# Row maxima of dense attention: two heads' products of 64 rows beside each other in the array, one reduction over two banks

## The chip, the cores and the metric

The kernel runs on one core of a Trainium2 chip. The metric is the device time of one execution in microseconds. A core has five engines that run side by side and wait for each other by semaphores: TensorE (PE in the profile; its weight loads are listed apart as PEld), VectorE (DVE), ScalarE (ACT), GpSimd (POOL) and SyncE (SP). Each takes its instructions in the order in which the program lists them. DMA transfers are issued by SP or by POOL, and then run by themselves.

## The reference, cut to what matters

One layer of an encoder over 1024 positions: a projection, two kinds of attention side by side, an output projection and a gated feed-forward part. The change lies in the dense attention (8 query heads in two groups of 4; each group shares one key head of 64 elements):

```
def block(qb):
    sc = jnp.einsum('bqkgd,bskd->bkgqs', qb, k, preferred_element_type=jnp.float32) * scale
    p = jax.nn.softmax(sc, axis=-1)
    return jnp.einsum('bkgqs,bskd->bqkgd', p.astype(v.dtype), v)
o = lax.map(block, qg)
```

A softmax gives the same result whatever is taken off all scores of a row. The kernel takes off an approximate maximum of the row, so that the exponentials stay in range; the maximum itself is not part of the output.

## The kernel before, in words

The work runs in stages: the input projection in four chunks of columns, the dense attention, the windowed attention, the output projection, and the feed-forward part. Operands of TensorE are in a 4-byte format that keeps fewer digits than float32; so a number is split into a high part and a low part, and a product is made of up to three products of parts.

Dense attention is worked in 16 groups: 8 blocks of 128 queries by 2 key heads (`a_main`, from line 594 on). A group has 4 query heads, and goes over the 1024 keys in 8 key tiles of 128. For each key tile there are two 512-column products for the scores (L609 with the keys, high parts over low parts in the 128 rows, against the queries; L610 with the high parts of the keys and rows of -1 against the low parts of the queries and the row maxima, which subtracts them), an exponential on ACT (L612), and four products in float32 with the values (L604, each of which shows as two records in the trace), two key tiles later.

The row maxima of a group have to be there before its scores, so they are made one group ahead, by the steps of `a_prep` (from line 567 on), of which `a_main` takes one behind most key tiles (`plan`, line 1006). The first step transposes the queries of the group into `q2`: their high parts stand in rows 0 to 63 and again in rows 64 to 127. Then come four steps `mx(i)`, one for each head, and `last`, which joins the maxima of the two halves of the keys and transposes them into the operand of L610. In `R_K2A` the rows 0 to 63 hold the high parts of the keys and the rows 64 to 127 their low parts. So the product of L582 is the high part of the queries times the whole of the keys, 128 rows deep, with 512 keys in one bank of the accumulator memory. Each bank is reduced to a maximum for each row by one DVE instruction (L583). The first group uses four banks in turn; the others, which share the memory with the scores, use banks 0 and 1.

The operands of the keys are made in `k_ready` (lines 315 to 327) during the last chunk of the projection: `kv_fetch` loads the keys, ACT and DVE split them (L319, L320), TensorE transposes them (L176), and ACT copies them to `R_K2A` (L326) and their high parts alone to rows 0 to 63 of `R_KHA` (L327). The rows 64 to 127 of `R_KHA` hold -1. In the loop over the 28 products of the projection (L393 to L395 are its three products of parts), `k_ready` of the last keys is called behind the product that is called 6, and the four `mx` of the first group behind the product that is called 3. A scheduler then sets the order of each engine's instructions by the dependencies and by its own notion of how long things take. So the `mx` of the first group end up between the projection's products, and those of the other groups between the products of scores and values. POOL works in the same stretch on additions of the projection's outputs (L405), rotary steps (L284), and the loads of two tables (L648).

## Time and profile before

| what | us |
|---|---|
| median of 3 runs (1378.29 to 1380.36) | 1379.73 |
| the profiled execution | 1379.28 |
| its span from first to last instruction | 1377.5 |
| PE busy in the span | 1319.2 |
| the products of the maxima (L582) start from, to | 228.6, 434.1 |
| the reductions (L583) start from, to | 230.0, 434.6 |

The dense stage is some 205 of the span's 1377.5 us. A row of a group gives the line, the engine, the operation, output and input with their shapes, the count, the busy time, the mean length in ns of one, and then the idle time of the engine ahead of these instructions with what ended it. A row in order of time gives the start, the length, the engine, the line and the count; the lengths of products are modelled and overlap, so what a product takes is read from the distance of the starts.

### The profile page before, as it was taken

The numbers are of one execution on the slowest core, as the hardware profiler recorded it, in microseconds if no ns is written. First come the engines' busy times: TensorE is split into PE (matmuls) and PEld (weight loads), VectorE is DVE, ScalarE is ACT, GpSimd is POOL, SyncE is SP. The second block draws the span as 40 slices with busy tenths as digits, with TensorE's granted clock in tenths as the row PEclk, the third lists the DMA queues.
The fourth block names the chain that finished last, engine by engine and source line by source line (L and its number), as shares of the span: only waits on it lengthen the run. The fifth ranks groups of instructions, "written<-read, shape, count | busy, mean of one in ns | idle before, by whom it ended". The sixth has DMA issues, their size and how long they took to land.

```text
span 1377.5 us, 20282 instructions
## 1 busy us (share of the span) xinstructions
PE 1319.2 (96%) x7559; PEld 1141.6 (83%) x7559; DVE 988.2 (72%) x1634; ACT 671.5 (49%) x1066; POOL 515.3 (37%) x388
## 2 busy tenths in 40 slices
PE   7898989999999999999998999999999999999998
PEld 6798989989999887887886788888888888888887
DVE  5986586774445677688558888778777888586664
ACT  7744634554445656666344444444444445244331
POOL 2754354130001566651036455665565552200000
PEclk9999999999999999989999999999999999999999
DMA  7035303100000223234322222333223225797973
GB/s 245 16 116 138 78 9 87 30 9 1 1 1 9 83 71 102 82 109 137 107 70 84 91 94 92 102 112 112 103 100 115 85 100 176 280 293 239 295 232 112
DMA packets 117956, 148.61 MB, mean 108 GB/s; under 512 B 48809, under 2 KB 74849, under 8 KB 117857
## 3 DMA queue, kind: packets, MB, share of 16 engines
q1 hardware_dynamic: 116705, 144.17, 32.2%
q0 software_dynamic: 1152, 3.15, 0.9%
q8 instruction: 59, 0.97, 0.3%
q14 instruction: 40, 0.33, 0.1%
HBM read 113.47 MB, written 33.82 MB: 107 GB/s over the span
## 4 chain that ended last, share of the span: by engine, by line
PE 75%; DVE 12%; issue 3%; ACT 2%; POOL 1%; DMA 1%; DVEq 0%; ACTq 0%; SPq 0%; POOLq 0%
PE ps L1123 10%; PE ps L1124 9%; PE ps L1125 9%; PE ps L604 7%; PE ps L1239 5%; PE ps L1237 5%; PE ps L1238 5%; PE ps L609 2%; PE ps L582 2%; PE ps L847 2%; DVE bigf L707 2%; PE ps L610 2%; PE ps L849 2%; PE ps L848 2%; PE ps L393 2%
## 5 line engine op out<-in xcount | busy, mean ns | idle before, releaser
L1123 PE MATMUL ps<-bigr 128*128 128x512 f32 x616 | 241.7, 392 | 6.1 <-DVE bigf L1127 5.8
L1125 PE MATMUL ps<-bigr 128*128 128x512 f32 x616 | 240.5, 390 | 0.0
L1124 PE MATMUL ps<-bigr 128*128 128x512 f32 x616 | 240.2, 390 | 0.0
L1106 ACT ACTIVATE bigr<-bigf 128x512 fp32r<-128x512 f32 x154 | 93.0, 625 | 157.3 <-POOL bigf L1098 97.5
L1155 DVE SCALAR_TENSOR_TENSOR bigf<-bigf 128x768 f32<-128x768 f32 (+1 forms) x176 | 145.5, 885 | 27.0 <-ACT bigf L1153 27.0
L604 PEld LDWEIGHTS ps<-bigf 128*128 128x128 f32 x1024 | 138.7, 191 | 10.1
L1123 PEld LDWEIGHTS ps<-bigr 128*128 128x128 f32 x616 | 115.9, 188 | 34.5 <-DVE bigf L1127 10.0
L1217 ACT ACTIVATE bigr<-bigf 128x1024 fp32r<-128x1024 f32 x77 | 80.7, 1060 | 119.4 <-PE ps L1239 65.6
L393 PE MATMUL ps<-bigr 128*128 128x256 f32 x448 | 128.9, 288 | 7.8 <-ACT bigf L408 5.2
L1125 PEld LDWEIGHTS ps<-bigr 128*128 128x128 f32 x616 | 116.1, 188 | 24.3
L1107 DVE TENSOR_TENSOR bigr<-bigf,bigr 128x512 fp32r<-128x512 f32 x110 | 113.1, 1043 | 31.3 <-ACT bigr L1106 31.2
L1124 PEld LDWEIGHTS ps<-bigr 128*128 128x128 f32 x616 | 116.0, 188 | 23.5
L604 PE MATMUL ps<-bigf 128*128 128x65 f32 x1024 | 135.3, 267 | 0.0
L583 DVE TENSOR_REDUCE bigf<-ps 128x1 f32<-128x512 f32 x128 | 85.8, 689 | 64.7 <-PE ps L582 63.1
L394 PE MATMUL ps<-bigr 128*128 128x256 f32 x448 | 128.3, 287 | 0.0
L395 PE MATMUL ps<-bigr 128*128 128x256 f32 x448 | 128.1, 286 | 0.0
L612 ACT ACTIVATE bigf<-ps 128x512 f32<-128x512 f32 x128 | 76.0, 597 | 101.3 <-PE ps L610 99.7
L1238 PE MATMUL ps<-bigr 128*128 128x512 f32 x308 | 119.9, 389 | 0.0
L1237 PE MATMUL ps<-bigr 128*128 128x512 f32 x308 | 119.8, 389 | 0.0
L1239 PE MATMUL ps<-bigr 128*128 128x512 f32 x308 | 119.8, 389 | 0.0
L1218 DVE TENSOR_TENSOR bigr<-bigf,bigr 128x1024 fp32r<-128x1024 f32 x77 | 93.0, 1221 | 26.9 <-ACT bigr L1217 24.8
L1169 POOL TENSOR_TENSOR bigf<-bigf 128x512 f32<-128x512 f32 x44 | 69.1, 1591 | 90.3 <-DVE bigf L1160 66.0
(209 smaller groups left out, 3048.4 us busy)
## 6 DMA issues: line engine op xcount, KB each, us to landing
bigf<-w_down SPq DMA_DIRECT2D x99, 256.0 KB, 4.1
bigf<-w_up SPq DMA_DIRECT2D x44, 512.0 KB, 3.6
bigf<-gscr SPq DMA_DIRECT2D x77, 256.0 KB, 4.3
gscr<-bigf SPq DMA_DIRECT2D x33, 512.0 KB, 2.6
bigf<-w_in SPq DMA_DIRECT2D x8, 1024.0 KB, 6.7
bigf<-x SPq DMA_DIRECT2D x15, 512.0 KB, 8.0
bigf<-tmx SPq DMA_DIRECT2D x8, 672.0 KB, 5.0
bigf<-w_out SPq DMA_DIRECT2D x8, 512.0 KB, 3.6
```

The costliest lines, as they stand in the source:

```text
L393: mm(o, ah, wh, start=(k == 0 and t % 2 == 0 and n != 2), stop=False, skip_group_check=True)
L394: mm(o, ah, wl, start=False, stop=False, skip_group_check=True)
L395: mm(o, al, wh, start=False, stop=(k == 3), skip_group_check=True)
L604: mm(bank(ob, 65, 66 * i), f(slots[kt] + 128 * i, 128), f(F_VA + 132 * kt + 66 * kv, 65), start=(kt == 0 and i == 0), stop=(kt == 7), skip ...
L1107: (gp if n in (2, 4) else vec).tensor_tensor(rp(o + 512, [128, 4], [1, 128]), src, rfp(o, [128, 4], [1, 128]), op=OP.subtract)
L1123: mm(bank(b), wh, th, start=(k == 0 and n in (1, 5, 6, 7)), stop=False, skip_group_check=True)
L1124: mm(bank(b), wh, tl, start=False, stop=False, skip_group_check=True)
L1125: mm(bank(b), wl, th, start=False, stop=(k == 3), skip_group_check=True)
L1155: vec.scalar_tensor_tensor(f(a + o, n), f(i + d, n), w_, f(a + o, n), op0=OP.mult, op1=OP.add)
L1237: mm(o, ah, r(d, 512), start=(q == 0 and n in (1, 5, 2)), stop=False, skip_group_check=True)
L1238: mm(o, ah, r(d + 1024, 512), start=False, stop=False, skip_group_check=True)
L1239: mm(o, al, r(d, 512), start=False, stop=(q == NQ - 1), skip_group_check=True)
```

## The change

The step `mx(i)` is made anew. It now takes a pair of heads and one half of the keys. It issues two products of 64 rows: one with rows 0 to 63 of `q2` for the first head of the pair and rows 0 to 63 of `R_K2A`, the other with rows 64 to 127 of `q2` for the second head (where the same high parts stand again) and rows 64 to 127 of a new operand `R_KK`. Both use the high parts of the keys alone. They write two neighbouring banks, and one reduction over both gives two maxima for each row. The count of products stays 128, that of the reductions goes from 128 to 64. `R_KK` is filled by a copy of 512 KB, from rows 0 to 63 of `R_KHA` to rows 64 to 127, on POOL's queue, behind the last `k_ready`.

```
+R_KK = R_KHA + 2048
...
         def mx(i):
-            for hf in range(2):
-                b = 2 * (i % 2) * (g == 0) + hf
-                mm(bank(b), r(q2 + 128 * i, 128), r(R_K2A + 1024 * kv + 512 * hf, 512), start=True, stop=True)
-                vec.tensor_reduce(f(SM_MC + 8 * hf + i, 1), bank(b), axis=AX.X, op=OP.max)
+
+            pair, hf = divmod(i, 2)
+            b = 2 * (i % 2) * (g == 0)
+            for u, k in ((0, R_K2A), (1, R_KK)):
+                rows = slice(64 * u, 64 * u + 64)
+                mm(bank(b + u), r(q2 + 128 * (2 * pair + u), 128)[rows], r(k + 1024 * kv + 512 * hf, 512)[rows],
+                   start=True, stop=True)
+            vec.tensor_reduce(f(SM_MC + 8 * hf + 2 * pair, 2), heads(PS[:, 512 * b:512 * b + 1024], 2), axis=AX.X,
+                              op=OP.max)
...
             for u in range(2, 4):
                 k_ready(u)
                 v_ready(u)
+            gp.dma_start(r(R_KK, 2048)[64:128], r(R_KHA, 2048)[0:64])
```

The order of instructions changes at three places. Lines of the changed kernel lie 1 higher than those of before up to the dense stage's `a_prep` and 6 higher behind it (7 behind the copy): L394 to L396 are the projection's products (L393 to L395 before), L586 is the product of a maximum (L582), L615 and L616 are the scores (L609 and L610), L610 the product with the values (L604), L406 and L285 are L405 and L284.

The first place is PE near the end of the projection, where the first group's maxima stand. Before, around the second and third step of the maxima:

```order
L394 MATMUL ps<-bigr 128x256
L582 MATMUL ps<-bigr 128x512 [waits DVE_49]
L582 MATMUL ps<-bigr 128x512
L395 MATMUL ps<-bigr 128x256
L393 MATMUL ps<-bigr 128x256
L582 MATMUL ps<-bigr 128x512 [waits DVE_49]
```

In the changed kernel, around the second product of the first pair; the semaphore named DMASW0 is that of POOL's DMA queue:

```order
L394 MATMUL ps<-bigr 128x256
L586 MATMUL ps<-bigr 128x512 [waits DMASW0_49]
L586 MATMUL ps<-bigr 128x512 [waits DVE_49,Activation_49]
L586 MATMUL ps<-bigr 128x512
L395 MATMUL ps<-bigr 128x256
L396 MATMUL ps<-bigr 128x256
```

The first product of the first pair stands ten projection products ahead of these rows, at the place where the first two L582 stood before; the second product has moved behind those ten, and now waits for the copy, and the rest of the projection's products stand behind it.

The second place is POOL at the same time. Before, behind the two additions of the projection's outputs:

```order
L477 TENSOR_TENSOR bigf<-bigf 128x512 [waits DVE_49,Pool_49]
L405 TENSOR_TENSOR bigf<-bigf 128x4x256 [waits DVE_49]
L405 TENSOR_TENSOR bigf<-bigf 128x4x256 [waits Activation_49]
L284 TENSOR_TENSOR bigf<-bigf 128x8x16 [waits DVE_49,Pool_49]
L284 TENSOR_TENSOR bigf<-bigf 128x8x16
```

In the changed kernel:

```order
L478 TENSOR_TENSOR bigf<-bigf 128x512 [waits DVE_49,Pool_49]
L406 TENSOR_TENSOR bigf<-bigf 128x4x256 [waits DVE_49]
L406 TENSOR_TENSOR bigf<-bigf 128x4x256 [waits Activation_49]
L996 DMA bigr<-bigr 64x2048 [waits PE_49,Activation_49]
L285 TENSOR_TENSOR bigf<-bigf 128x8x16 [waits DVE_49,Pool_49]
```

The copy (L996) stands behind both additions, and ahead of the rotary steps; nothing else on POOL has moved here.

The third place is PE in a later group of the dense stage. Before, from one step of the maxima on:

```order
L582 MATMUL ps<-bigr 128x512
L604 MATMUL ps<-bigf 128x65 x2
L582 MATMUL ps<-bigr 128x512
L604 MATMUL ps<-bigf 128x65 x2
L609 MATMUL ps<-bigr 128x512
L610 MATMUL ps<-bigr 128x512
L582 MATMUL ps<-bigr 128x512
L604 MATMUL ps<-bigf 128x65 x2
```

In the changed kernel, from one pair to the next:

```order
L586 MATMUL ps<-bigr 128x512 x2
L615 MATMUL ps<-bigr 128x512
L616 MATMUL ps<-bigr 128x512
L610 MATMUL ps<-bigf 128x65 x4
L615 MATMUL ps<-bigr 128x512
L616 MATMUL ps<-bigr 128x512
L610 MATMUL ps<-bigf 128x65
L586 MATMUL ps<-bigr 128x512 x2
```

Before, the two products of a step mostly stood apart, with products of the values between them; now the two of a pair stand together, with two score products twice and five products of the values (ten records) up to the next pair.

## The prediction

> **What bounds the kernel now.** I read the page first, then the busy time by stretches of the span, then the instructions in order of time in the dense stage, and last the groups and waits of the lines that the change touches. The page gives the engines for the whole span; the stretches (columns: from:to, length, then busy time and count of PE, PEld, DVE, ACT and POOL, granted clock, DMA share, GB/s) tell the stages apart.

> ```profile
> PE 1319.2 (96%) x7559; PEld 1141.6 (83%) x7559; DVE 988.2 (72%) x1634; ACT 671.5 (49%) x1066; POOL 515.3 (37%) x388
> 260.00:300.00 40.00, 39.50 (x281) 35.91 (x281) 31.80 (x54) 23.58 (x38) 8.93 (x3) 1.00 0.01 2
> 300.00:340.00 40.00, 40.00 (x289) 36.67 (x288) 21.36 (x38) 18.83 (x33) 2.38 (x2) 1.00 0.03 8
> 340.00:380.00 40.00, 40.00 (x288) 36.63 (x288) 19.02 (x37) 18.82 (x33) 0.00 (x0) 1.00 0.01 1
> ```

> The dense stage is bound by TensorE alone: PE is busy for all of 300 to 380 at full clock, while DVE works half of it. Here the weight loads (PEld) are close behind, at 92%. So a saving on DVE is worth nothing here, and one on PE is worth its whole size. One stretch of PE in order of time shows what a maximum costs (start, length, engine, line):

> ```profile
> 300.89 0.48 PE L609 MATMUL ps<-bigr 128*128 128x512 f32 x1
> 301.21 0.40 PE L582 MATMUL ps<-bigr 128*128 128x512 f32 x1
> 301.44 0.39 PE L610 MATMUL ps<-bigr 128*128 128x512 f32 x1
> 301.67 1.00 PE L604 MATMUL ps<-bigf 128*128 128x65 f32 x8
> 302.48 0.48 PE L609 MATMUL ps<-bigr 128*128 128x512 f32 x1
> 302.80 0.39 PE L610 MATMUL ps<-bigr 128*128 128x512 f32 x1
> 303.03 1.00 PE L604 MATMUL ps<-bigf 128*128 128x65 f32 x8
> 303.83 0.48 PE L609 MATMUL ps<-bigr 128*128 128x512 f32 x1
> ```

> Start to start is what a product takes from PE; the lengths overlap. The key tile from 300.89 to 302.48 holds one maximum product (L582) and takes 1.59 us; the next, from 302.48 to 303.83, has none and takes 1.35. So one product costs 0.24 us, though its modelled length is 0.39, and two cost 0.48. A record of L604 takes 0.10 (eight in 0.81). The first 512-column product behind them takes 0.32 instead of 0.23, about 0.1 more: its own weight load was not hidden.

> **The change part by part.**

> *The reductions.* 128 of one bank become 64 of two:

> ```profile
> L583 DVE TENSOR_REDUCE bigf<-ps 128x1 f32<-128x512 f32 x128 | 85.8, 689 | 64.7 <-PE ps L582 63.1
> L464 DVE TENSOR_REDUCE bigf<-bigf 128x16 f32<-128x1024 f32 x4 | 4.8, 1212 | 0.0
> 301.64 0.69 DVE L583 TENSOR_REDUCE bigf<-ps 128x1 f32<-128x512 f32 x1 [0.66 <-PE ps L582]
>   DVE bigf L583: 2.7, 6
> ```

> The last row is of the products' own line: PE sat idle ahead of L582 for 2.7 us, 6 times, until a reduction had ended. A reduction over 1024 elements takes 1.21 us on another line, so 64 of them take 77.6 us against 88.2 (128 x 0.689): 10.6 us less on an engine that waited 63.1 us for these very products. Worth nothing on the path. On the other side, both banks now come free together, at 0.43 (product's start to reduction, 301.21 to 301.64) + 0.1 + 1.21 = 1.75 us behind a pair's start. In the new order two pairs have some 2.1 us of other PE work between them (two L609, two L610 and ten L604 by the lines of before), so no wait follows. Where DVE is fuller, at 260 to 300, PE may wait longer than the 2.7 us that it lost to reductions before; I take 0, and keep 2.7 more as the bound.

> *The products.* Their number stays 128, but each uses 64 of the array's rows, in two halves. If the halves stream together, a pair takes 0.24 instead of 0.48, and 64 pairs save 64 x 0.24 = 15.4 us. What stands against it is that every neighbour of a pair uses all 128 rows, so the array changes its division into a pair and out of it again: about 128 times. The trace of before has one such change, at its start, where a transposition of 8 rows (L512) follows those of 128 rows:

> ```profile
> 6.04 0.42 PE L179 MATMUL ps<-bigf 128*128 128x128 f32 x1
> 6.39 0.18 PEld L512 LDWEIGHTS ps<-bigf 8*128 8x128 f32 x1 [0.33 <-issue]
> 6.39 0.27 PE L512 MATMUL ps<-bigf 8*128 8x8 f32 x1
> 5.83 0.23 PEld L179 LDWEIGHTS ps<-bigf 128*128 128x128 f32 x1
> 5.83 0.63 PE L179 MATMUL ps<-bigf 128*128 128x128 f32 x2
> 16.58 1.04 PE L179 MATMUL ps<-bigf 128*128 128x128 f32 x8
> ```

> The weights of the product at 6.04 had been loaded from 5.83 on, ahead of it. Those of L512 were not loaded ahead: they began at 6.39, 0.35 us behind the start of the product before and 0.07 before its modelled end at 6.46, and the profile names nothing else that L512 waited for. It is a single event, at a place where the kernel has just begun, but the nearest row there is. Carried over to a 512-column product with a length of 0.39: the next weights start at 0.32, a load takes about 0.1, and the next product streams at 0.42 or 0.43 instead of 0.23 or 0.24. That is a hold of 0.19 at each change. A pair then costs 0.24 for the stream, 0 to 0.10 for the second half's weights, and 2 x 0.19: 0.62 to 0.72 against 0.48, so 0.14 to 0.24 more. Times 64: 9 to 15 us; I take 12. The change pays only if a hold is under about 0.1 us.

> [...]

> *The copy of the keys.* It is issued on POOL behind two additions, and PE's order has the second product of the first pair wait for it, with all of PE's later work behind.

> ```profile
> 223.12 5.81 POOL L405 TENSOR_TENSOR bigf<-bigf 128x1024 f32<-128x1024 f32 x2 [5.65 <-DVE bigf L405]
> DMA to landing us min/median/max: 3.7/4.1/4.4
> bigf<-w_up SPq DMA_DIRECT2D x44, 512.0 KB, 3.6
> bigf<-x SPq DMA_DIRECT2D x15, 512.0 KB, 8.0
> 228.61 0.63 PE L582 MATMUL ps<-bigr 128*128 128x512 f32 x2
> 229.08 0.28 PE L393 MATMUL ps<-bigr 128*128 128x256 f32 x1
> 229.19 0.27 PE L394 MATMUL ps<-bigr 128*128 128x256 f32 x1
> ```

> The two additions end at 223.12 + 5.81 = 228.93, so the copy can't be issued earlier, though the keys themselves are ready before. The only loads on POOL's queue, L648 with 384 KB, land in 3.7 to 4.4 us (second row); loads of 512 KB on the other queue take 3.6 (w_up) to 8.0 (x, in a crowd at the start). No copy from on-chip memory to on-chip memory is in the trace. With 4.1 it lands at 233.0. PE is at the first pair at 228.61; one product (0.24) and ten projection products at 0.12 later, at about 230.05, it stands at the product that waits. It is idle until 233.0: 3.0 us, from 2.5 to 6.8 by the other rows. What was late before is no cover, since PE ran without a gap through this place. The reductions of this group follow as they did, and end (four of 1.21) before PE needs their result behind some 40 more projection products. Behind the copy on POOL stand the rotary steps L284 and the table loads; half a microsecond of issue there delays nothing that PE waits for.

> A pause on PE can also cost clock:

> ```profile
> 203.42 0.54 PE L176 MATMUL ps<-bigr 128*128 128x128 f32 x4 [1.71 <-DVE bigr L320]
> 207.55 0.72 PE L176 MATMUL ps<-bigr 128*128 128x128 f32 x4 [3.60 <-DVE bigf L191]
> 208.41 0.41 PE L394 MATMUL ps<-bigr 128*128 128x256 f32 x1
> 208.63 0.41 PE L395 MATMUL ps<-bigr 128*128 128x256 f32 x1
> 208.00:212.00 4.00, 4.00 (x21) 4.00 (x20) 3.35 (x6) 2.45 (x5) 0.44 (x1) 0.50 0.25 66
> ```

> After gaps of 1.71 and 3.60 us the granted clock was 0.50, and some 20 products came 0.21 apart (208.41 to 208.63) instead of 0.12: about 2 us. One gap of 3.0 is shorter than that, so I take 0 and keep 2 as a bound.

> *Sum.* The profiled execution took 1379.28 us with a span of 1377.5; the median of the runs is 1379.73, 0.45 above it. 1379.28 + 12 for the changes of division + 3.0 for the copy = 1394 us. The case's own range: 1379.3 + 9 + 2.5 = 1391 at its low end, and 1379.3 + 15 + 6.8 + 2 + 2.7 = 1406 with every bound at once.

> **The rivals.**

> *The halves stream together and a change of division costs nothing.* Faster. For it: the weights of a half could load while the other half streams, and the product before a pair is a 512-column one in about half of the places, long enough for both loads. Price: -15.4 + 3.0 = 1367 us; with 0.10 per pair for the second half's weights, -9.0 + 3.0 = 1373. Take 1370. Against it: the row of L512. It decides from a hold under 0.1 us per change, and at 0.07 the gain just pays for the copy: 64 x (0.24 - 0.05 - 0.14) = 3.

> *The halves do not overlap.* Then the change doesn't do what it says: each 64-row product takes 0.24 as before, without a hold, and only the copy is left: 1382 us, 0.2% slower. For it: nothing in this trace shows two products at once. Against it: nothing either.

> *The hold is that of L512 in full,* 0.35 at each change on top of the stream and the loads (0.10 each): 0.24 + 0.10 + 2 x 0.35 = 1.04 per pair, 0.56 more, 64 x 0.56 + 3 = 39 us: 1418. Against it: the transpositions there started 0.21 apart (5.83 and 6.04), while later eight of them take 1.04 in all, 0.1 apart, so that stretch ran slow.

> **How the numbers follow.** Forecast (holds of about 0.19 and the copy): 0.53, around 1394. Free changes of division: 0.29, around 1370. No overlap and no hold: 0.08, around 1382. Full hold: 0.06, around 1418. Holds of 0.07 or so, which about cancel: 0.04, around 1380. The range from 1367 to 1406 takes in the first, the second and those between, and leaves out the full hold and the crossing of several bounds. About 0.2% is what a measurement of this kernel can tell from no change, 2.8 us. Faster by more: 0.29. Within it: the cancelling case and part of the no-overlap case, 0.07. Slower: 0.64.

> **What would show it right or wrong.** In the profile after: the weight loads of each pair, and those of the product behind it, start only near the modelled end of the product before, 0.3 us and more behind its start; key tiles with a pair take 0.6 to 0.7 us more than those without, not 0.24; a gap of about 3 us in PE near 230, ended by the copy; DVE's reductions at about 1.2 us and DVE no busier. The prediction is wrong if the second product of a pair starts within hundredths of the first and the next full product 0.24 later (first rival), if the products of a pair are 0.24 apart with no hold (second), or if the copy has landed before PE asks for it.

## The result, and the profile after

| | before | changed |
|---|---|---|
| median, us | 1380.05 | 1457.72 |
| lowest of the runs, us | 1378.29 | 1457.24 |
| profiled execution, us | 1379.28 | 1457.24 |
| its span, us | 1377.5 | 1455.5 |
| mean granted clock of TensorE | 0.988 | 0.942 |

The changed kernel is slower: ratio 1.0562, interval 1.0547 to 1.0578, which is 77.7 us. The forecast was 1394, with a range up to 1406: the sign is right, the size is not. (One of the four executions of the changed kernel took 1569.5 us at a mean clock of 0.866 and is left out of the ratio.)

The page of the changed kernel, engines and granted clock in 40 slices:

```profile
PE 1390.2 (96%) x7559; PEld 1181.9 (81%) x7559; DVE 981.4 (67%) x1570; ACT 674.1 (46%) x1066; POOL 514.7 (35%) x389
PEclk9999997555799999999999999999999999999999
```

PE's share of the span is 96% as before, with the same 7559 instructions. By the busy share alone nothing has happened. The second row tells what has: from the seventh slice on, five slices of 36 us each with a lower clock, three of them at half clock throughout. Before, no slice is under 8. The stretches of the dense stage of the changed kernel, cut where the granted clock changes and at two round places (the clock is the third number from the right):

```profile
205.20:212.00 6.80, 5.03 (x25) 5.06 (x26) 5.41 (x13) 5.08 (x10) 1.03 (x1) 0.50 0.12 39
232.50:242.70 10.20, 9.98 (x39) 8.01 (x40) 4.97 (x5) 0.00 (x0) 1.15 (x2) 0.50 0.24 61
249.60:382.70 133.10, 132.47 (x490) 108.49 (x491) 48.84 (x65) 39.00 (x63) 15.93 (x15) 0.50 0.04 10
340.00:380.00 40.00, 40.00 (x152) 33.15 (x152) 9.17 (x13) 10.06 (x18) 0.00 (x0) 0.50 0.00 1
382.70:460.00 77.30, 77.30 (x534) 64.67 (x532) 33.07 (x44) 35.40 (x60) 0.00 (x0) 1.00 0.00 1
420.00:460.00 40.00, 40.00 (x279) 33.71 (x277) 18.01 (x24) 17.47 (x30) 0.00 (x0) 1.00 0.00 1
```

The stretch at 205.2 is there before as well (6.8 us from 205.7). The other two are new: 10.2 us from 232.5, and 133.1 us from 249.6. In 40 us at half clock PE issues 152 products, at full clock 279 (before: 288). PE is "busy" for all of both.

Where the 77.7 us lie in the kernel is told by the exponentials, which run through the whole dense stage (lengths, then the first and the last start). Before, and then in the changed kernel:

```profile
L612 ACT ACTIVATE bigf<-ps x128: 582/597/602, 239.4 to 453.1; 128x512 f32<-128x512 f32 x128
```

```profile
L618 ACT ACTIVATE bigf<-ps x128: 589/597/602, 246.6 to 529.8; 128x512 f32<-128x512 f32 x128
```

Up to the first exponential 7.2 us are lost, from the first to the last 283.2 - 213.7 = 69.5, and behind the last 1455.5 - 529.8 - (1377.5 - 453.1) = 1.3. That is the whole difference of the spans, 78.0. The loss is in the stage that the change is in, and in what leads up to it.

Next, the price of the change at full clock. DVE joins the maxima once in each group; the distance of two joins is the time of a group. Before, and then in the changed kernel behind 382.7:

```profile
327.88 0.17 DVE L586 TENSOR_TENSOR bigr<-bigf 128x4 fp32r<-128x4 f32 x1
341.33 0.17 DVE L586 TENSOR_TENSOR bigr<-bigf 128x4 fp32r<-128x4 f32 x1
```

```profile
429.69 0.17 DVE L592 TENSOR_TENSOR bigr<-bigf 128x4 fp32r<-128x4 f32 x1
443.71 0.17 DVE L592 TENSOR_TENSOR bigr<-bigf 128x4 fp32r<-128x4 f32 x1
```

13.45 against 14.02 (13.43 over several groups of before): 0.59 more in a group, 0.147 for each of its four pairs, 9.4 us in 16 groups. (The line numbers differ between the kernels: the join is L586 before and L592 in the changed kernel, where L586 is the product of a pair.) PE in order of time shows both halves of it in the changed kernel:

```profile
427.48 0.48 PE L615 MATMUL ps<-bigr 128*128 128x512 f32 x1
427.88 0.51 PE L586 MATMUL ps<-bigr 64*128 64x512 f32 x2
428.32 0.50 PE L616 MATMUL ps<-bigr 128*128 128x512 f32 x1
```

A score product is followed by the pair 0.40 later where 0.23 to 0.24 is the stream, and the pair by the next score product 0.44 later: about 0.17 and 0.20 of hold, and the two products of the pair share one 0.24. The pair's row of 0.51 holds two products of 0.50 each, so they start within about 0.01 us of each other.

The copy, its wait, and the reductions over two banks:

```profile
222.57 5.80 POOL L406 TENSOR_TENSOR bigf<-bigf 128x1024 f32<-128x1024 f32 x2 [5.78 <-DVE bigf L406]
228.32 0.73 POOL L996 DMA_DIRECT2D bigr<-bigr  x1
DMA to landing us min/median/max: 4.4/4.4/4.4
232.72 1.22 PE L586 MATMUL ps<-bigr 64*128 64x512 f32 x3 [2.72 <-DMA bigr<-bigr]
PE ps L586 <- DVE bigf L588: 1.1, 1, 1.1
L588 DVE TENSOR_REDUCE bigf<-ps 128x2 f32<-128x1024 f32 x64 | 78.3, 1224 | 133.0 <-PE ps L586 132.9
```

The copy was issued behind the two additions, took 4.4 us to land, and PE sat idle for 2.72 us. A reduction takes 1.224 us, and PE waited for one once, for 1.1 us. With a wait of 0.9 for an exponential, shown further down, that is 2.0 us beside the copy, against 0.8 before. So the holds and the copy of the forecast's sum are there and of about their size, and some 60 to 64 us beside them are clock.

### The profile page after: what moved, and what is told of

Same layout as the page of the kernel before. It is cut to its first block, busy times and chain, and to the rows that moved or that the text cites. A ratio compares the mean times of both kernels' runs of the same rounds, so it can differ in the third digit from the quotient of the medians.

```text
span 1455.5 us, 20221 instructions
## 1 busy us (share of the span) xinstructions
PE 1390.2 (96%) x7559; PEld 1181.9 (81%) x7559; DVE 981.4 (67%) x1570; ACT 674.1 (46%) x1066; POOL 514.7 (35%) x389
## 4 chain that ended last, share of the span: by engine, by line
PE 69%; DVE 14%; issue 4%; POOL 3%; ACT 3%; DMA 1%; DVEq 0%; ACTq 0%; SPq 0%; POOLq 0%
PE ps L610 10%; PE ps L1130 7%; PE ps L1131 7%; PE ps L1132 7%; PE ps L1244 5%; PE ps L1245 5%; PE ps L1246 5%; PE ps L615 3%; PE ps L616 3%; DVE bigf L1162 3%; PE ps L586 2%; PE ps L853 2%; DVE bigf L713 2%; PE ps L855 2%; PE ps L854 2%
## 5 line engine op out<-in xcount | busy, mean ns | idle before, releaser
L610 PEld LDWEIGHTS ps<-bigf 128*128 128x128 f32 x1024 | 170.8, 236 | 20.1 <-issue 9.0
L610 PE MATMUL ps<-bigf 128*128 128x65 f32 x1024 | 169.1, 314 | 0.0
L588 DVE TENSOR_REDUCE bigf<-ps 128x2 f32<-128x1024 f32 x64 | 78.3, 1224 | 133.0 <-PE ps L586 132.9
L394 PE MATMUL ps<-bigr 128*128 128x256 f32 x448 | 130.5, 292 | 7.8 <-ACT bigf L409 5.2
L395 PE MATMUL ps<-bigr 128*128 128x256 f32 x448 | 130.1, 291 | 0.0
L396 PE MATMUL ps<-bigr 128*128 128x256 f32 x448 | 129.5, 289 | 0.0
## 6 DMA issues: line engine op xcount, KB each, us to landing
bigf<-w_up SPq DMA_DIRECT2D x44, 512.0 KB, 3.5
gscr<-bigf SPq DMA_DIRECT2D x33, 512.0 KB, 2.6
bigf<-x SPq DMA_DIRECT2D x15, 512.0 KB, 8.4
bigf<-w_out SPq DMA_DIRECT2D x8, 512.0 KB, 3.6
```

Source lines behind the costliest of these rows:

```text
L394: mm(o, ah, wh, start=(k == 0 and t % 2 == 0 and n != 2), stop=False, skip_group_check=True)
L395: mm(o, ah, wl, start=False, stop=False, skip_group_check=True)
L396: mm(o, al, wh, start=False, stop=(k == 3), skip_group_check=True)
L610: mm(bank(ob, 65, 66 * i), f(slots[kt] + 128 * i, 128), f(F_VA + 132 * kt + 66 * kv, 65), start=(kt == 0 and i == 0), stop=(kt == 7), skip ...
```

## The experiments

The first question was what sends the clock down; the second, what keeps it there for 133 us. My first theory was the pause for the copy; the rivals were the wait behind a two-bank reduction, and something in the pairs themselves.

**The copy made early.** In four parts on SP's queue, each behind the keys that it copies, so that it has landed long before PE asks:

```
     def k_ready(u):
...
+        dma(rfp(R_KK + 256 * u, [1024, 2], [1, 256])[64:128], rfp(R_KHA + 256 * u, [1024, 2], [1, 256])[0:64])
...
-            gp.dma_start(r(R_KK, 2048)[64:128], r(R_KHA, 2048)[0:64])
```

> The changed kernel, with the copy of the keys made in four parts on SP's queue, each behind the step that makes its keys, so that it has landed before PE asks for it. Theory 1 (the pause of 2.7 us for the copy is what sends the clock down, and the stage then stays down): without it the dense stage runs at full clock, about 1380 + 12 = 1392 us. Theory 2 (the clock falls at 246 to 250 for another reason, PE waiting for a two-bank reduction that stands behind other DVE work, and the stage cannot bring it up again): only the pause and the first stretch at half clock are gone, 2.7 + up to 5 us: 1450 to 1455 us, with the clock at 0.50 up to about 380.

The profiled execution took 1431.38 us; three others took 1564.72, 1555.07 and 1564.0 at mean clocks of 0.868 to 0.872. In the profiled one (a wait of PE, then stretches):

```profile
241.66 0.80 PE L587 MATMUL ps<-bigr 64*128 64x512 f32 x2 [1.16 <-DVE bigf L589]
237.88:241.30 3.42, 1.86 (x11) 1.45 (x11) 2.06 (x2) 2.71 (x6) 2.08 (x5) 1.00 0.00 0
241.00:333.00 92.00, 91.34 (x335) 74.41 (x336) 39.30 (x52) 28.56 (x45) 15.92 (x15) 0.50 0.06 14
```

PE no longer waits for the copy, and the clock goes down all the same, at 241.3, in the waits at the start of the first group's scores. It comes up after 92.2 us. So the pause is not what makes the long stretch, and how long it lasts differs from execution to execution of one kernel. That the three longer executions stayed at half clock through the stage is an estimate from their mean clock, for there is no trace of them: in the longest, 2 x (1 - 0.868) x 1563 us of span gives some 413 us at half clock, and 16 groups of 25.45, the length of a group at half clock in a later run, are 407.

**Two-bank reductions alone.** The products are those of before (128 rows deep, both parts of the keys); no copy.

```
-            for u, k in ((0, R_K2A), (1, R_KK)):
-                rows = slice(64 * u, 64 * u + 64)
-                mm(bank(b + u), r(q2 + 128 * (2 * pair + u), 128)[rows], r(k + 1024 * kv + 512 * hf, 512)[rows],
+            for u in range(2):
+                mm(bank(b + u), r(q2 + 128 * (2 * pair + u), 128), r(R_K2A + 1024 * kv + 512 * hf, 512),
                    start=True, stop=True)
...
-            gp.dma_start(r(R_KK, 2048)[64:128], r(R_KHA, 2048)[0:64])
```

> The two-bank reduction alone: pairs of heads and one reduction over two banks as in the changed kernel, but products 128 rows deep with high and low parts of the keys as before, and no copy. Theory 2 in its strong form (the wait for the two banks lowers the clock, and no form of this stage brings it up again): clock 0.50 for a good part of the stage, 1430 us or more. If the 64-row products are needed for the stage to stay down: 1380 to 1385 us, full clock but for a window or two.

1384.08 us, ratio 1.0041 (1.0025 to 1.0057): 5.4 us. The longest two of PE's waits among the first scores, the stretches that they lie in, and two joins in later groups:

```profile
239.03 0.53 PE L614 MATMUL ps<-bigr 128*128 128x512 f32 x1 [0.89 <-ACT bigf L617]
242.04 0.73 PE L585 MATMUL ps<-bigr 128*128 128x512 f32 x2 [1.14 <-DVE bigf L587]
237.60:241.00 3.40, 2.42 (x17) 1.77 (x14) 1.37 (x2) 3.39 (x6) 2.06 (x6) 1.00 0.03 8
241.00:244.45 3.45, 2.41 (x16) 2.19 (x17) 3.41 (x3) 0.60 (x1) 2.40 (x5) 1.00 0.31 79
305.88 0.17 DVE L591 TENSOR_TENSOR bigr<-bigf 128x4 fp32r<-128x4 f32 x1
319.31 0.17 DVE L591 TENSOR_TENSOR bigr<-bigf 128x4 fp32r<-128x4 f32 x1
```

A later group takes 13.43 us, as before, so the two-bank reduction costs nothing in the steady part. It costs in the first three groups: up to 285 us PE waits six times, for reductions, exponentials and a join, 4.05 us together (0.26 in the kernel before). The kernel before hardly waits around its first scores:

```profile
229.00:245.00 16.00, 15.64 (x109) 13.63 (x107) 12.92 (x20) 6.40 (x10) 7.45 (x13) 1.00 0.30 69
```

That is 0.36 of idle time, where the two rows of the two-bank form have 0.98 + 1.04. The clock stays at 1.00 all the same, with these waits split over two stretches; what this does not settle is said below.

**The pause alone.** The kernel before, with one product of the first step reading a copy of its own operand, made on POOL's queue at the place of the change's copy:

```
+                k = R_KK if g == 0 and i == 0 and hf == 1 else R_K2A + 1024 * kv + 512 * hf
...
+            gp.dma_start(r(R_KK, 512), r(R_K2A + 512, 512))
```

> The kernel before, with one product of the first group's maxima reading its keys from a copy that is issued on POOL at the place of the change's copy (256 KB), so that PE pauses there for some 2.5 us. Nothing else differs. If a pause is enough to send the stage of before down for long: over 1420 us. If the stage of before comes up again by itself: 1380 + 2.5 + up to 3 at half clock = 1383 to 1386 us.

1383.44 us, ratio 1.0034 (1.0021 to 1.0046). The wait, and the stretch around it:

```profile
231.20 0.50 PE L584 MATMUL ps<-bigr 128*128 128x512 f32 x1 [2.44 <-DMA bigr<-bigr]
229.49:232.90 3.41, 1.70 (x11) 1.61 (x12) 1.66 (x3) 0.00 (x0) 2.02 (x3) 1.00 0.32 94
```

A pause of 2.44 us costs 4.8 by the medians (1383.44 - 1378.67), and no half clock follows it. What the rest of the 4.8 is was not traced.

**A burst of dense products.** The changed kernel with 24 products of 128 rows by 512 columns in the third group, whose results nothing uses:

```
             take(late, late_plan[kt])
+            if g == 2 and kt == 6:
+                for j in range(24):
+                    mm(bank(j % 2), r(q2, 128), r(R_K2A, 512), start=True, stop=True)
```

> The changed kernel with 24 more 512-column products of 128 rows, back to back, in the third group (their results are not used). They cost 16 x 0.43 at half clock and 8 x 0.22 at full, 8.6 us. If the stage stays down only because nothing in it is dense enough to bring the clock up, the burst brings it up and it then holds: the stretch at 0.50 ends near 300 instead of 382, some 80 us at half clock fewer are worth 35 to 40 us, and the time is 1425 to 1432 us. If the pairs themselves hold the clock down, it falls again within a few windows: 1462 to 1467 us.

1433.2 us, ratio 1.0396 (1.0372 to 1.0419): 24.5 us less than without the extra work. Products of the burst, and stretches ahead of it and behind:

```profile
315.52 2.91 PE L623 MATMUL ps<-bigr 128*128 128x512 f32 x6
318.69 4.87 PE L623 MATMUL ps<-bigr 128*128 128x512 f32 x18
300.00:319.00 19.00, 19.00 (x70) 15.90 (x70) 10.33 (x14) 3.18 (x7) 10.40 (x4) 0.50 0.07 15
340.00:480.00 140.00, 140.00 (x961) 116.91 (x960) 59.49 (x79) 64.25 (x110) 0.00 (x0) 1.00 0.00 1
```

The clock comes up at 319.8, in the burst, and then stays up with the very pairs under which it had stayed down for 71.7 us. So the same stage ran at two lasting speeds, half clock ahead of the burst and full clock for the 140 us behind it.

**The early copy and the burst together.** The edit of the first experiment, with the burst at `g == 1 and kt == 3`:

> The changed kernel with the early copy, and 24 more 512-column products of 128 rows back to back in the second group, which bring the clock up early (their results are not used). If pairs hold the full clock once they have it, the stage runs at 14.02 us per group to its end: 16 x 0.59 = 9.4 us for the changes of division, 5 to 8 for the burst, 3 to 6 for waits on banks and one or two windows at half clock, 1379 + 9.4 + 13 = 1397 to 1404 us. If they fall again by themselves: over 1420 us.

1411.42 us, ratio 1.0235 (1.0218 to 1.0252), and all four executions lie within 1.3 us of each other. A stretch ahead of the drop, and two joins at full clock:

```profile
241.69:245.10 3.41, 2.24 (x14) 1.64 (x14) 3.41 (x4) 0.98 (x2) 2.03 (x4) 1.00 0.19 42
398.30 0.17 DVE L593 TENSOR_TENSOR bigr<-bigf 128x4 fp32r<-128x4 f32 x1
412.32 0.17 DVE L593 TENSOR_TENSOR bigr<-bigf 128x4 fp32r<-128x4 f32 x1
```

The clock is down for 34.1 us from 245.1, until the burst; then groups of 14.02 us to the end. Its time is a sum: 1379.5, + 9.4 for the holds, + 24 x 0.24 = 5.8 for the burst, + half of 34.1 for the clock, is 1411.8. That it agrees within half a microsecond is in part luck: at 25.45 us a group instead of 14.02, the figure of a later run, 34.1 us lose 15.3 and not 17.1, and PE's waits (2.5 us here, 0.8 before) are not in the sum.

**Both products in the same half.** No copy; both products of a pair in rows 0 to 63, with the burst. If the halves don't stream together, this costs nothing beside the two halves.

```
-            for u, k in ((0, R_K2A), (1, R_KK)):
-                rows = slice(64 * u, 64 * u + 64)
+            for u in range(2):
+                rows = slice(0, 64)
...
```

> As the run with the early copy and the burst, but both products of a pair use rows 0 to 63, so that they cannot stream beside each other; no copy is needed. If the halves of the changed kernel do stream together, a pair here costs one product more: 0.21 to 0.24 us, 14.02 + 4 x 0.22 = 14.9 us per group, 15 us more over the stage than the run with the halves. If they don't stream together there, the periods are equal. The order at full clock matters; a stretch at half clock is left out.

1426.84 us, ratio 1.0345 (1.0324 to 1.0365). The joins:

```profile
422.47 0.17 DVE L592 TENSOR_TENSOR bigr<-bigf 128x4 fp32r<-128x4 f32 x1
437.40 0.17 DVE L592 TENSOR_TENSOR bigr<-bigf 128x4 fp32r<-128x4 f32 x1
```

14.93 a group: 0.91 more than with two halves, 0.228 a pair, which is the stream of one product. So the halves do stream together, all but fully. Against before it is 1.50 a group, 0.375 a pair: two holds of 0.19 on average, with nothing else to see.

**A stall of PE at full clock.** To see how each kind of stage comes back from half clock, PE is made to wait some 12 us in a later group, by a chain on DVE ahead of the join that it needs:

```
         def last():
+            if g == 10:
+                j = f(O_F + 7840, 352)
+                vec.tensor_copy(j, f(SM_MC, 1).to_broadcast([128, 352]))
+                for _ in range(30):
+                    vec.tensor_tensor(j, j, j, op=OP.max)
+                vec.tensor_copy(f(SM_MC, 1), f(O_F + 7840, 1))
```

In the kernel before:

> The kernel before with a chain of 30 small DVE operations ahead of the step that joins the maxima of the eleventh group, so that PE has nothing to do for some 6 to 9 us in the middle of the stage and its clock falls. Nothing of the stage's own work is changed. If the stage of before brings its clock up by itself: the stall and one or two windows at half clock, 1379 + 7 to 13 = 1386 to 1392 us, and group periods of 13.4 us again behind it. If any form of this stage stays down once it is down: six groups at some 25 us instead of 13.4, 1440 us or more.

1395.91 us, ratio 1.012 (1.01 to 1.0141). The stretches of the stall, behind it, and later:

```profile
377.00:387.00 10.00, 0.00 (x0) 0.00 (x0) 9.38 (x19) 0.00 (x0) 0.00 (x0) 0.50 0.00 0
387.00:397.00 10.00, 9.31 (x31) 7.58 (x32) 4.81 (x10) 3.51 (x6) 0.00 (x0) 0.50 0.01 2
398.00:440.00 42.00, 42.00 (x304) 38.60 (x302) 20.56 (x39) 18.64 (x33) 0.00 (x0) 1.00 0.00 1
```

PE works again from 387.7, and the clock is up at 397.3: some 10 us of work at half clock, and it is over.

With the pairs (the kernel of the early copy and the burst):

> The changed kernel with the early copy and the early burst (1411 us by itself, at full clock from the fourth group on), and the same stall in the eleventh group as in the two runs before. If the clock of this stage comes up again as it does in the kernel before, in about three windows of 3.4 us of work: 1411 + 16 = 1427 us. If the pairs keep it down: the five groups behind the stall take 20 to 27 us each instead of 14, 1450 to 1490 us.

1484.92 us, ratio 1.0764 (1.0737 to 1.0792). The stretches ahead of the stall and behind it, and two joins behind it:

```profile
340.00:400.00 60.00, 60.00 (x413) 50.00 (x413) 28.81 (x41) 27.18 (x47) 0.00 (x0) 1.00 0.00 1
419.00:480.00 61.00, 61.00 (x228) 50.80 (x228) 14.65 (x18) 14.91 (x26) 0.00 (x0) 0.50 0.00 1
483.41 0.17 DVE L599 TENSOR_TENSOR bigr<-bigf 128x4 fp32r<-128x4 f32 x1
508.85 0.17 DVE L599 TENSOR_TENSOR bigr<-bigf 128x4 fp32r<-128x4 f32 x1
```

The clock goes down at 406.9 and is down for 143.4 us, with PE busy all through behind the stall; a group takes 25.45 us. It comes up in the last group, 18 us behind the last pair. The same stall costs the kernel before 16 us and this one 73.5 (1484.92 - 1411.42). This is the main finding: at full clock the pairs cost 9.4 us in all; what costs the rest is that the stage with them gets the full clock back late (after 92.2 and 133.1 us above) or, as here, not while they run.

With the holds, but with products of 128 rows. The kernel before, with a product of 64 rows and 8 columns ahead of the first product of each step, in the bank that this one then overwrites, and the stall:

```
             for hf in range(2):
                 b = 2 * (i % 2) * (g == 0) + hf
+                if hf == 0:
+                    mm(bank(b, 8), r(q2 + 128 * i, 128)[0:64], r(R_K2A + 1024 * kv, 8)[0:64], start=True, stop=True)
```

> The kernel before with one more product of 64 rows and 8 columns ahead of the first product of each step of the maxima (its result is overwritten), and the stall in the eleventh group. All products of before keep their 128 rows; only the changes of division are added, four in and out per group. Their price at full clock, 4 x 2 x 0.19 = 1.5 us per group and some 0.1 per small product: 13.43 + 1.5 to 1.9 = 14.9 to 15.3 us. If the holds keep the clock down: 1380 + 28 + 40 or more, 1450 us. If not: 1380 + 28 + 16 = 1424 us.

1419.27 us, ratio 1.0288 (1.0268 to 1.0309). Two joins at full clock, and the stretches behind the stall:

```profile
336.62 0.17 DVE L594 TENSOR_TENSOR bigr<-bigf 128x4 fp32r<-128x4 f32 x1
351.59 0.17 DVE L594 TENSOR_TENSOR bigr<-bigf 128x4 fp32r<-128x4 f32 x1
401.00:412.00 11.00, 10.69 (x36) 8.48 (x36) 4.51 (x9) 3.58 (x7) 0.00 (x0) 0.51 0.00 0
412.00:470.00 58.00, 58.00 (x389) 49.83 (x388) 23.59 (x46) 24.30 (x42) 0.00 (x0) 1.00 0.00 1
```

14.97 a group, 1.54 more than before: 0.385 a step, which is two holds of at most 0.19, since the small product's own time is in it. Yet the clock is up after the same 10 us of work as without them (401.3 to 411.7). Holds of this size alone didn't keep it down here.

With half of the maxima's products left out (the kernel before, looking at the first 512 keys alone):

```
-            for hf in range(2):
-                b = 2 * (i % 2) * (g == 0) + hf
+            for hf in range(1):
+                b = i % 2
...
-            vec.tensor_tensor(rp(R_QLN + 512 * kv + 64, [128, 4]), f(SM_MC, 4), f(SM_MC + 8, 4), op=OP.max)
+            vec.tensor_tensor(rp(R_QLN + 512 * kv + 64, [128, 4]), f(SM_MC, 4), f(SM_MC, 4), op=OP.max)
```

> The kernel before with half of the maxima's products (only the first 512 keys are looked at for the shift of a row), and the same stall in the eleventh group as in the other run with a stall. There are then as many streams of 512 columns per group as in the changed kernel, but no change of division. If what keeps the clock down is only that fewer columns stream: six groups at some 23 us behind the stall, 1400 us or more. If it is the changes of division or the halves: 12.5 us per group throughout, 1364 + 7 to 13 = 1371 to 1377 us.

1389.1 us, ratio 1.0071 (1.0051 to 1.0091). Behind the stall:

```profile
371.00:401.00 30.00, 27.67 (x105) 24.35 (x106) 7.33 (x16) 8.66 (x15) 0.00 (x0) 0.50 0.00 1
```

The clock comes up by itself, but after about 28 us of work (373.1 to 401.8) and not 10.

With both products in the same half, and the stall:

> Both products of a pair in rows 0 to 63, early burst (1427 us by itself), and the stall in the eleventh group. As many columns stream as in the kernel before, but through 64 rows and with the changes of division. If the count of streaming columns decides: up again in some three windows, 1427 + 16 = 1443 us. If the halves or the changes of division keep it down: 1460 us or more.

1449.32 us in one execution and 1499.4 in the other. In the first:

```profile
423.00:450.00 27.00, 25.59 (x88) 20.23 (x88) 6.60 (x10) 7.58 (x13) 0.00 (x0) 0.50 0.00 1
```

Down for 37.5 us, the last 26 of them with PE at work, then up; the other execution lost 50 us more, and there is no trace of it. So it is inconclusive as a comparison, but it shows products of 64 rows that do let the clock come up, once of two times, with only one half of the rows in use.

**Half of the maxima, without the stall.** The last edit but one by itself is a version to compare with both kernels:

> The kernel before with half of the maxima's products: the shift of a row comes from the first 512 keys alone, in products of 128 rows and reductions of one bank. No change of division. In the run with the stall its groups took 12.50 us at full clock against 13.43, so 16 x 0.93 = 15 us less than before: 1364 to 1366 us, at full clock throughout.

1364.51 us, ratio 0.9888 (0.9871 to 0.9904): it beats both. 64 products fewer, at the forecast's 0.24 each, are 15.4 us; the medians differ by 15.38 (1379.89 in the same series). What is taken off a row's scores is not part of the output, so the kernel computes the same function; but the exponentials of the other 512 keys are then not held to a range by a maximum of their own, so it is a choice that the data must allow.

## Why the prediction went wrong, point by point

| term | forecast, us | the runs | from |
|---|---|---|---|
| holds at the changes of division | +12 (9 to 15) | +9.4 | groups of 13.43 and 14.02 |
| pause for the copy | +3.0 (2.5 to 6.8) | +2.7 | PE's wait in the trace |
| waits behind two-bank reductions | 0 (to 2.7) | +1.3 to +5.4 | PE's waits in the trace, 2.0 less 0.8 before; the reductions alone |
| clock | 0 (to 2) | about +60 to +64 | what is left of 77.7 |

- **The step that failed** is the one on the clock: "One gap of 3.0 is shorter than that, so I take 0 and keep 2 as a bound." It fails twice over. The gap of 2.72 alone sent the clock down at 232.5, for 10.2 us (with the copy made early the clock stays up there, to 241.3); a pause of 2.44 in the kernel before did not. And the bound assumed that a stage comes up within some 20 products, as the projection does. Behind the next drop, at 249.6, the stage with the pairs needed 133.1 us. The size fits: at half clock a group of pairs takes 25.45 us instead of 14.02, so the work of 133.1 us would have taken 133.1 x 14.02 / 25.45 = 73.3 at full clock. That is 59.8 lost there, and up to half of 10.2 before it.
- **Holds: right.** 0.19 at each change was read from one row at the start of the kernel; two experiments give 0.375 and 0.385 for the two changes of a step. That so close a figure came from one product of 8 rows, among products that started 0.21 apart instead of 0.1, is in part luck. At full clock the pair costs 0.147 more, at the low end of 0.14 to 0.24; the second half's weights cost nothing visible.
- **The halves stream together: right.** 0.228 a pair is lost when they can't. So the first rival was half right, and falls with the holds; the second (no overlap, no hold) falls on both counts; the third (0.35 at each change) is nearly twice the size measured.
- **Copy: right**, 4.4 to land and 2.72 of idle time against 4.1 and 3.0.
- **Reductions: right that the 10 us on DVE are worth nothing; too low at the edge.** In the steady part there is no wait. The two-bank form alone costs 5.4 us, twice the bound, and 4.05 of it are PE's waits in the first three groups: 1.5 in the stretch from 260 on that the forecast named, and 2.6 ahead of it. The bound itself came from a misread row: of the 2.7 us, 6 times, ahead of L582, 1.9 are gaps of the weight loads, listed along with PE's, and PE itself waited 0.8, twice.
- **What would have shown it wrong.** The list named the places of the holds and of the copy, and these are as foreseen; the two products of a pair also start within hundredths, as the first rival would have it, with the holds around them. It named no row of the clock. The granted clock of each stretch was there to read in the profile of before, and the changed stage's need to win it back was not asked for.

What stands ahead of the drop at 249.6, in the trace of the changed kernel (a wait of PE, and the stretch that it lies in):

```profile
247.23 0.50 PE L615 MATMUL ps<-bigr 128*128 128x512 f32 x1 [0.89 <-ACT bigf L618]
246.20:249.60 3.40, 2.00 (x13) 1.46 (x11) 1.78 (x2) 2.98 (x6) 2.06 (x5) 1.00 0.00 0
```

PE is idle for 1.4 of these 3.4 us. The wait for the exponential is the same 0.89 us that the reductions alone have, and behind it comes the wait for a reduction (1.15 here, ended at 250.24; 1.14 there); before has neither. So the two-bank reductions bring these waits, and the early copy shows that they come, and the clock goes down, without the pause. With products of 128 rows the same waits lowered no clock (the reductions alone), but there they fall into two stretches, with 0.98 and 1.04 of idle time, so that run alone does not show that the 64-row products have a part in the drop. A stretch of the same-half run with the stall speaks for it: from 409.1 to 412.5 it has only 0.75 of idle time (2.66 of 3.41 busy), and half clock follows. That the waits are what lowers the clock with the pairs is argued from the time at which it happens; the pairs with one-bank reductions were not tried.

**What stays open** is what decided in these runs whether the clock went down or came up. PE's busy time over 3.4 us does not tell the cases apart: stretches with 2.66 of 3.41 busy (the one just named), 2.24 (early copy and burst) and 2.00 (changed) were followed by half clock, those with 1.70 (pause alone), 2.41 and 2.42 (reductions alone) were not; and stretches that were busy throughout (40.00 of 40.00 us from 340 on in the changed kernel) didn't bring the clock up. The stages that did come up within 10 us have eight products of 512 columns over 128 rows in each group beside the scores; with four of them it took 28 us; with eight over 64 rows, all in one half, 26 us or far more; and with eight over 64 rows in both halves it took 92.2 and 133.1 us, or came 18 us behind the last of them. Which of rows, columns and halves decides was not measured by itself.

## What to carry to other kernels

Behind a wait, the stage of before won back the full clock after some 10 us of work, the one with half of its maxima's products after 28, and the one with the pairs after 92 and 133 us, or only behind the last pair. So for a change that gives TensorE products of fewer rows or fewer columns, ask first whether the stage still wins back the full clock after an ordinary wait; read the granted clock stage by stage in the profile after, since PE's busy share, 96% before and after, showed nothing of it. Two products of 64 rows did share one stream (0.228 us a pair are lost when they can't), but a lone pair between products of 128 rows pays 0.38 us of holds to save 0.24: by these figures two pairs in a row would save 0.48 for the same holds, an estimate that was not tried. A product that isn't needed at all was worth its whole 0.24 (15.38 us for 64).
